# A separate block of minus ones for the norm's second matmul, at an address 16 bytes past the others, and 15 KB less scratch ahead of the tiles

## Chip, core and metric

The kernel runs on one core of a Trainium2 chip. The metric is device microseconds (us) of one execution, the median of several runs. One further execution was taken with the hardware profiler; all rows below come from it. The engines are PE (TensorE, with PEld for its weight loads), DVE (VectorE), ACT (ScalarE), POOL (GpSimd) and SP (SyncE, which here issues the transfers).

## What is computed

A decoder trunk of four layers on 256 tokens of width 1024, in float32. Each layer is a half-weighted gated feed-forward block, a token mixer (three kinds in turn), and a second half-weighted feed-forward block. Each block starts with an RMS norm. The reference, cut:

```python
def rms_norm(x, g):
    y = x * lax.rsqrt(jnp.mean(x * x, axis=-1, keepdims=True) + EPS)
    return y * g

def swiglu(x, w_gate_up, w_down):
    g, u = jnp.split(x @ w_gate_up, 2, axis=-1)
    return (jax.nn.silu(g) * u) @ w_down

for i in range(4):                                   # D_MODEL 1024, D_FF 2816
    h = h + 0.5 * swiglu(rms_norm(h, norm_ffn1[i]), ffn1_w_gate_up[i], ffn1_w_down[i])
    hn = rms_norm(h, norm_mix[i])
    h = h + (stick_breaking, moba, mla)[i % 3](hn)
    h = h + 0.5 * swiglu(rms_norm(h, norm_ffn2[i]), ffn2_w_gate_up[i], ffn2_w_down[i])
return rms_norm(h, final_norm)
```

## The kernel before

**Split operands.** Every large matrix product is made of three products of rounded parts. A weight chunk is loaded by SP into a `raw` tile, ACT writes its rounded high part into one of six `whi` tiles (L318), DVE writes the rest, the low part, into one of six slots of the tile `wlo` (L325). The activations are split in the same way: `x2` holds, for each of 8 blocks of 128 features, 256 high and then 256 low values a row; `a2` holds the same for the 22 blocks of the feed-forward block's inner width.

**The wide pair.** In the feed-forward blocks the three products are two matmuls (function `wide`, L475 and L476). The first holds a high weight block of 128x128 in the array and streams 512 columns, the high and low activations side by side. The second holds the low weight block and streams the 256 high columns. A feed-forward block has 22 x 16 such pairs in its gate-and-up part (`gate_up`) and 8 x 22 in its down part, 528 in all, and there are eight blocks: 4224 pairs. While one matmul streams, the array's next weight block is loaded (PEld).

**Other products.** The mixers' projections use three matmuls of 256 columns (`mm3`, L469 to L471, weights high, high, low), or three of up to 512 columns in which the activations are the held operand (`x_proj`, L516 to L518).

**The norm of a feed-forward block** (`norm_rows`). ACT and DVE split the sum of squares `acc` into a high and a low half, `parted`, the last block of `a2`. PE then sums over the 128 partitions with a block of minus ones: L441 streams all 512 columns, L442 streams the 256 low columns once more, both with the same block `full` held. DVE takes the inverse root from the result (L447 to L453). The pair L441, L442 stands in PE's order some 24 pairs after the start of a feed-forward block, since a block's first products need the norm only when they leave PSUM. There are eight such pairs in the program. `full` is also held in the stick-breaking mixer (L667).

**Addresses.** [...] In the built program `whi` starts at byte 49280, `full` at 73856, `x2` at 74432, `a2` at 90816, `wlo` at 135872: each a multiple of 64. The six low slots, however, begin 4 values, 16 bytes, into `wlo`:

```python
lows = cp.tile([P, 4 + 6 * HALF], F32R, name="wlo")
parts = Slots([(whi[i], lows[:, 4 + i * HALF:4 + (i + 1) * HALF]) for i in range(6)])
```

So a high weight block, `full` and all streamed rows begin at a multiple of 64 bytes, and a low weight block begins 16 bytes past one. A block of 128 values is 512 bytes, so in each slot the blocks lie 512 bytes apart.

**Order.** A small scheduler (class `Program`) fixes the order of the instructions on each engine when the kernel is built, from costs written in the code.

Of the kernel before, what the change touches and what calls it, by code (L numbers as in the profile page):

```python
# [11 lines left out]
F32R = mybir.dt.float32r  # L12
# [3 lines left out]
ALU = mybir.AluOpType  # L16
AX = mybir.AxisListType

P = 128
D = 1024  # L20
SEQ = 256
# [18 lines left out]
HALF = MAXC // 2  # L40
# [155 lines left out]
def trunk_kernel(ctx: ExitStack, tc: tile.TileContext, a: dict, out: bass.AP, nsub: int = 3 * DEPTH):  # L196
    nc = tc.nc
    ctx.enter_context(tc.manual_schedule())
    cp = ctx.enter_context(tc.tile_pool(name="consts", bufs=1))
# [21 lines left out]
    def room(n, shape, name, dt=F32):  # L221
        return Slots([cp.tile([P] + shape, dt, name=f"{name}{i}") for i in range(n)])
# [5 lines left out]
    whi = [cp.tile([P, HALF], F32R, name=f"whi{i}") for i in range(6)]  # L228
    full = cp.tile([P, P], F32R, name="full")
# [1 line left out]

    x2 = cp.tile([P, NT, 2, SEQ], F32R, name="x2")
    a2 = cp.tile([P, NF, 2, SEQ], F32R, name="a2")
    lows = cp.tile([P, 4 + 6 * HALF], F32R, name="wlo")
    parts = Slots([(whi[i], lows[:, 4 + i * HALF:4 + (i + 1) * HALF]) for i in range(6)])
    mids = room(3, [2 * ZC], "mid")
    probs = room(2, [2, ZC], "prob")
    nats = room(5, [512], "nat")
# [20 lines left out]
    def bank(keep=0):  # L259
        return Buf(psum, keep)  # L260
# [10 lines left out]
    identf = cp.tile([P, P], F32, name="identf")  # L271
# [9 lines left out]
    nc.vector.tensor_scalar(neg_sb, jp, 0.0, NEG, op0=ALU.is_le, op1=ALU.mult)  # L281
    nc.vector.tensor_scalar(neg_sm, jp, 0.0, NEG, op0=ALU.is_gt, op1=ALU.mult)
    nc.vector.tensor_scalar(tri, jp, 0.0, -1.0, op0=ALU.is_le, op1=ALU.mult)
    nc.vector.tensor_scalar(full, identf, 0.0, -1.0, op0=ALU.mult, op1=ALU.add)
    nc.vector.memset(onesf, 1.0)


# [137 lines left out]
    def norm_rows():  # L425


        t, z = Buf(mids), bank()
        lead = 10.0

        parted = a2[:, NF - 1].rearrange("p a b -> p (a b)")
        th, tl, tx = (slice(i * SEQ, (i + 1) * SEQ) for i in range(3))

        def high():
            nc.scalar.activation(parted[:, th], acc, AF.Copy)

        def low():
            nc.vector.tensor_sub(parted[:, tl], acc, parted[:, th].bitcast(F32))

        def sums():  # L440
            nc.tensor.matmul(z.ap, full, parted, start=True, stop=False, skip_group_check=True)  # L441
            nc.tensor.matmul(z.ap[:, :SEQ], full, parted[:, tl], start=False, stop=True, skip_group_check=True)  # L442

        def newton():
            x, y, u = t.ap[:, tx], t.ap[:, th], t.ap[:, tl]

            nc.vector.tensor_scalar(x, z.ap[:, :SEQ], 0.5 / D, -0.5 * EPS, op0=ALU.mult, op1=ALU.add)  # L447
            nc.vector.tensor_scalar(y.bitcast(I32), x.bitcast(I32), -0.5, float(0x1EF759DF), op0=ALU.mult,
                                    op1=ALU.add)
            for i in range(3):  # L450
                nc.vector.tensor_mul(u, y, y)
                nc.vector.tensor_mul(u, u, x)
                nc.vector.scalar_tensor_tensor(rb[:, 0, :] if i == 2 else y, u, 1.5, y, op0=ALU.add, op1=ALU.mult)  # L453

        o = g.act(SEQ, high, [state["acc"]], lead=lead)
        o = g.dve(SEQ, low, [o], lead=lead)
        o = g.op("PE", wide_cost(1), sums, [o], take=[z, t], lead=lead)
        n = g.op("DVE", 11 * 0.4, newton, [o], free=[z, t], lead=lead)
        g.act(SEQ, lambda: nc.scalar.activation(rb[:, 1, :], rb[:, 0, :], AF.Copy, scale=0.5), [n], lead=lead)
        return n  # L460
# [17 lines left out]
    def wide_cost(n):  # L478
        return n * (3 * SEQ / 2400 + 0.005)
# [44 lines left out]
    def ffn(l, which, g_next):  # L524
        gu, dn = a[f"ffn{which + 1}_gu"], a[f"ffn{which + 1}_dn"]
        rms = norm_rows()
        act = [None] * NF
        xdeps = list(state["x"])
# [443 lines left out]
    for m, e in zip(CUTS, CUTS[1:] + [NT]):  # L972
        s = slice(G_ALL + m * SEQ if m else 0, G_ALL + e * SEQ)
        x = g.op("DMA", 0.37 * (e - m), lambda s=s: nc.sync.dma_start(gh[:, s], a["gx"][:, s]), lead=61.0 - 3.0 * m)
# [88 lines left out]
def build(arrays, nsub=3 * DEPTH):  # L1063
    import concourse.bacc as bacc

    nc = bacc.Bacc("TRN2", target_bir_lowering=False, num_devices=1)
    aps = {n: nc.dram_tensor(f"in_{n}", v.shape, mybir.dt.from_np(v.dtype), kind="ExternalInput").ap()
           for n, v in arrays.items()}
    out = nc.dram_tensor("out_0", (SEQ, D), F32, kind="ExternalOutput").ap()
    with tile.TileContext(nc) as tc:  # L1070
        trunk_kernel(tc, aps, out, nsub)
    return nc
# [9 lines left out]
```

## Time and profile before

| | |
|---|---|
| median of 3 runs | 1942.61 us (1941.03 to 1947.96) |
| the profiled execution | 1941.18 us |
| its span, from the first to the last instruction | 1939.3 us |
| mean granted TensorE clock | 0.996 of full speed |
| PE busy, share of the span | 1921.3 us, 99% |
| PEld / DVE / ACT / POOL busy | 87% / 76% / 59% / 0% |
| DMA, mean busy share of 16 engines, HBM read | 50.4% on its main queue, 339.76 MB |

Matmuls overlap: the next one starts while the one before still drains, so a matmul's duration (0.39 us for 512 columns) is longer than the distance to the next start. Rates are read from starts, or from how many matmuls of one line fall into a stretch.

### The profile page before, as it was taken

The numbers are of one execution on the slowest core, as the hardware profiler recorded it, in microseconds if no ns is written. First come the engines' busy times: TensorE is split into PE (matmuls) and PEld (weight loads), VectorE is DVE, ScalarE is ACT, GpSimd is POOL, SyncE is SP. The second block draws the span as 40 slices with busy tenths as digits, with TensorE's granted clock in tenths as the row PEclk, the third lists the DMA queues.
The fourth block names the chain that finished last, engine by engine and source line by source line (L and its number), as shares of the span: only waits on it lengthen the run. The fifth ranks groups of instructions, "written<-read, shape, count | busy, mean of one in ns | idle before, by whom it ended". The sixth has DMA issues, their size and how long they took to land.

```text
span 1939.3 us, 30483 instructions
## 1 busy us (share of the span) xinstructions
PE 1921.3 (99%) x11649; PEld 1683.4 (87%) x11649; DVE 1468.5 (76%) x2669; ACT 1149.3 (59%) x2119; POOL 0.4 (0%) x5
## 2 busy tenths in 40 slices
PE   8999999999999999999999999999999999999997
PEld 7888989888888878888888888988888888998886
DVE  8777668776877777877787778887678767668864
ACT  6565556555665555655566557755556655565553
POOL 0000000000000000000000000000000000000000
PEclk9999999999999999999999999999999999999999
DMA  7546434545654653454555454355465456335542
GB/s 277 196 150 228 167 138 155 193 155 193 217 196 147 226 183 119 161 206 150 199 208 192 154 183 155 127 199 178 154 217 199 173 175 230 131 132 194 182 151 80
DMA packets 55873, 342.77 MB, mean 177 GB/s; under 512 B 6192, under 2 KB 7088, under 8 KB 26928
## 3 DMA queue, kind: packets, MB, share of 16 engines
q1 hardware_dynamic: 55728, 340.84, 50.4%
q8 instruction: 91, 1.49, 0.3%
q14 instruction: 54, 0.44, 0.1%
HBM read 339.76 MB, written 1.05 MB: 176 GB/s over the span
## 4 chain that ended last, share of the span: by engine, by line
PE 98%; DVE 1%; ACT 1%; DMA 0%; issue 0%; SPq 0%; DVEq 0%; ACTq 0%
PE ps L475 50%; PE ps L476 25%; PE ps L469 3%; PE ps L470 3%; PE ps L471 3%; PE ps L516 3%; PE ps L518 2%; PE ps L517 2%; PE ps L615 1%; PE ps L665 1%; PE ps L774 1%; PE ps L739 1%; PE ps L812 1%; PE ps L637 1%; PE ps L603 0%; PE ps L617 0%
## 5 line engine op out<-in xcount | busy, mean ns | idle before, releaser
L318 ACT ACTIVATE whi<-raw 128x1024 fp32r<-128x1024 f32 (+2 forms) x738 | 703.4, 954 | 691.5 <-PE ps L475 486.3
L325 DVE TENSOR_TENSOR wlo<-raw,whi 128x1024 fp32r<-128x1024 f32 (+2 forms) x738 | 802.9, 1090 | 357.8 <-ACT whi L318 344.4
L475 PE MATMUL ps<-x,whi 128*128 128x512 f32 x2816 | 981.0, 394 | 0.7 <-DVE acc L349 0.6
L476 PE MATMUL ps<-x,wlo 128*128 128x256 f32 x2816 | 783.5, 278 | 4.3 <-DVE wlo L325 4.3
L475 PEld LDWEIGHTS ps<-x,whi 128*128 128x128 f32 x2816 | 529.4, 188 | 125.2 <-ACT whi L318 1.9
L476 PEld LDWEIGHTS ps<-x,wlo 128*128 128x128 f32 x2816 | 530.3, 188 | 5.1 <-DVE wlo L325 5.1
L475 PE MATMUL ps<-a,whi 128*128 128x512 f32 x1408 | 489.6, 394 | 0.0
L476 PE MATMUL ps<-a,wlo 128*128 128x256 f32 x1408 | 390.8, 278 | 0.0
L475 PEld LDWEIGHTS ps<-a,whi 128*128 128x128 f32 x1408 | 263.9, 187 | 61.3
L476 PEld LDWEIGHTS ps<-a,wlo 128*128 128x128 f32 x1408 | 264.3, 188 | 0.0
L484 DVE TENSOR_TENSOR mid<-ps,mid 128x256 f32<-128x256 f32 x416 | 172.7, 417 | 12.6 <-ACT mid L483 12.5
L483 ACT ACTIVATE mid<-ps 128x256 f32<-128x256 f32 x416 | 150.7, 366 | 11.4 <-PE ps L476 9.3
L556 DVE TENSOR_TENSOR mid<-mid 128x256 f32<-128x256 f32 x176 | 74.0, 423 | 11.7
L551 DVE TENSOR_TENSOR mid<-mid,rb 128x256 f32<-128x256 f32 x176 | 74.1, 423 | 4.8
L552 ACT ACTIVATE mid<-mid 128x256 f32<-128x256 f32 x176 | 72.0, 410 | 6.6 <-DVE mid L551 6.4
L558 DVE TENSOR_TENSOR a<-mid,a 128x256 fp32r<-128x256 f32 x176 | 73.1, 418 | 2.5 <-ACT a L557 2.4
L516 PE MATMUL ps<-whi,x 128*128 128x512 f32 (+2 forms) x192 | 74.0, 385 | 0.0
L469 PE MATMUL ps<-a,whi 128*128 128x256 f32 x256 | 73.8, 288 | 0.0
L469 PE MATMUL ps<-x,whi 128*128 128x256 f32 x256 | 73.1, 285 | 0.0
L518 PE MATMUL ps<-whi,x 128*128 128x512 f32 (+2 forms) x192 | 72.8, 379 | 0.0
L517 PE MATMUL ps<-wlo,x 128*128 128x512 f32 (+2 forms) x192 | 72.3, 377 | 0.0
L471 PE MATMUL ps<-x,wlo 128*128 128x256 f32 x256 | 71.9, 281 | 0.0
(141 smaller groups left out, 1658.0 us busy)
## 6 DMA issues: line engine op xcount, KB each, us to landing
raw<-in_ffn_gu SPq DMA_DIRECT2D x173, 1024.0 KB, 4.8
raw<-in_ffn_dn SPq DMA_DIRECT2D x128, 704.0 KB, 4.0
raw<-in_sb_qk SPq DMA_DIRECT2D x16, 1024.0 KB, 4.8
raw<-in_moba_qkv SPq DMA_DIRECT2D x12, 1024.0 KB, 4.8
raw<-in_sb_v SPq DMA_DIRECT2D x8, 1024.0 KB, 4.7
raw<-in_sb_o SPq DMA_DIRECT2D x8, 1024.0 KB, 4.7
raw<-in_moba_o SPq DMA_DIRECT2D x4, 1024.0 KB, 4.7
raw<-in_mla_o SPq DMA_DIRECT2D x4, 1024.0 KB, 5.0
```

The lines of the kernel that those rows point to most:

```text
L318: return lambda: nc.scalar.activation(b.ap[0][:, (k - i) * w:(e - i) * w], raw.ap[:, k * w:e * w], AF.Copy)
L325: nc.vector.tensor_sub(b.ap[1][:, s], raw.ap[:, k * w:e * w], b.ap[0][:, s].bitcast(F32))
L469: nc.tensor.matmul(o, wh, mh, start=first, stop=False, skip_group_check=True)
L471: nc.tensor.matmul(o, wl, mh, start=False, stop=last, skip_group_check=True)
L475: nc.tensor.matmul(o, wh, m2.rearrange("p a b -> p (a b)"), start=first, stop=False, skip_group_check=True)
L476: nc.tensor.matmul(o[:, :SEQ], wl, m2[:, 0, :], start=False, stop=last, skip_group_check=True)
L483: x = g.act(SEQ, lambda: nc.scalar.activation(o(), b.ap[:, SEQ:], AF.Copy), [last], take=take, lead=lead)
L484: return g.dve(SEQ, lambda: nc.vector.tensor_add(o(), b.ap[:, :SEQ], o()), [x], free=[b], lead=lead)
L516: nc.tensor.matmul(o, xs[0][:, k, ts], hi, start=(k == 0), stop=False)
L517: nc.tensor.matmul(o, xs[0][:, k, ts], lo, start=False, stop=False)
L518: nc.tensor.matmul(o, xs[1][:, k, ts], hi, start=False, stop=(k == n - 1))
L551: o = g.dve(SEQ, lambda: nc.vector.tensor_mul(x(), x(), rb[:, 0, :]), [o, rms])
```

## The change

Two things. The tile `wlo` becomes 128 values longer. Its first 128 values behind the 16 bytes are a second block of minus ones, `full_lo`, written once at the start by DVE; the six low slots move 512 bytes up. The norm's second matmul holds `full_lo` in place of `full`. And the framework's scratch area is set to 1 KB in place of 16 KB.

```diff
-    lows = cp.tile([P, 4 + 6 * HALF], F32R, name="wlo")
-    parts = Slots([(whi[i], lows[:, 4 + i * HALF:4 + (i + 1) * HALF]) for i in range(6)])
+    lows = cp.tile([P, 4 + P + 6 * HALF], F32R, name="wlo")
+    full_lo = lows[:, 4:4 + P]
+    parts = Slots([(whi[i], lows[:, 4 + P + i * HALF:4 + P + (i + 1) * HALF]) for i in range(6)])
...
-    nc.vector.tensor_scalar(full, identf, 0.0, -1.0, op0=ALU.mult, op1=ALU.add)
+    for x in (full, full_lo):
+        nc.vector.tensor_scalar(x, identf, 0.0, -1.0, op0=ALU.mult, op1=ALU.add)
...
             nc.tensor.matmul(z.ap, full, parted, start=True, stop=False, skip_group_check=True)
-            nc.tensor.matmul(z.ap[:, :SEQ], full, parted[:, tl], start=False, stop=True, skip_group_check=True)
+            nc.tensor.matmul(z.ap[:, :SEQ], full_lo, parted[:, tl], start=False, stop=True, skip_group_check=True)
...
-    nc = bacc.Bacc("TRN2", target_bir_lowering=False, num_devices=1)
+    nc = bacc.Bacc("TRN2", target_bir_lowering=False, num_devices=1, dynamic_dma_scratch_size=1024)
```

In the built program every tile up to and with the start of `wlo` lies 15,360 bytes lower, and every tile behind `wlo` 14,848 bytes lower; both are multiples of 512, so no tile's place within 512 bytes changes. Each low slot starts 14,848 bytes lower, 16 bytes past a multiple of 64 as before.

On PE the order of the instructions is the same. Here is the first norm's place in PE's order, before (the names after `<-` are the streamed tile and the held one, `ps` is a PSUM bank):

```order
L475 MATMUL ps_71<-x_86,whi_82 128x512
L476 MATMUL ps_71<-x_86,wlo 128x256
L441 MATMUL ps_72<-a_87,full 128x512
L442 MATMUL ps_72<-a_87,full 128x256
L475 MATMUL ps_70<-x_86,whi_82 128x512
L476 MATMUL ps_70<-x_86,wlo 128x256
```

And with the change, in which lines are numbered three higher here:

```order
L478 MATMUL ps_71<-x_86,whi_82 128x512
L479 MATMUL ps_71<-x_86,wlo 128x256
L444 MATMUL ps_72<-a_87,full 128x512
L445 MATMUL ps_72<-a_87,wlo 128x256
L478 MATMUL ps_70<-x_86,whi_82 128x512
L479 MATMUL ps_70<-x_86,wlo 128x256
```

Nothing moved; the second matmul of the norm reads its held block from `wlo`. The other seven norms read alike.

On DVE one instruction is added, among the constants that are written at the start. Before:

```order
L283 TENSOR_SCALAR tri<-acc 128x128
L284 TENSOR_SCALAR full<-identf 128x128
L285 MEMSET onesf 128x2
L360 SCALAR_TENSOR_TENSOR x_86<-gh,x_86 128x256
L325 TENSOR_TENSOR wlo<-raw_74,whi_78 128x256
```

With the change:

```order
L284 TENSOR_SCALAR tri<-acc 128x128
L286 TENSOR_SCALAR full<-identf 128x128
L286 TENSOR_SCALAR wlo<-identf 128x128
L287 MEMSET onesf 128x2
L362 SCALAR_TENSOR_TENSOR x_86<-gh,x_86 128x256
L327 TENSOR_TENSOR wlo<-raw_74,whi_78 128x256
```

The second L286 is new; everything behind it on DVE is one place later. ACT, POOL and SP have the same instructions in the same order.

## Rows read from the trace of the kernel before

**Rows 1.** The page's chain that ended last, by engine and by line.

```profile
PE 98%; DVE 1%; ACT 1%; DMA 0%; issue 0%; SPq 0%; DVEq 0%; ACTq 0%
PE ps L475 50%; PE ps L476 25%; PE ps L469 3%; PE ps L470 3%; PE ps L471 3%; PE ps L516 3%; PE ps L518 2%; PE ps L517 2%; PE ps L615 1%; PE ps L665 1%; PE ps L774 1%; PE ps L739 1%; PE ps L812 1%; PE ps L637 1%; PE ps L603 0%; PE ps L617 0%
```

**Rows 2.** L475 by stretch: stretch, its us, busy (matmuls), granted clock, DMA.

```profile
36.35:192.69 156.34, 156.34 (x460) 1.00 0.57 199
...
507.84:674.38 166.54, 166.54 (x490) 1.00 0.55 190
```

**Rows 3.** The same view, four other stretches.

```profile
321.20:507.70 186.50, 186.16 (x527) 1.00 0.53 186
801.30:989.20 187.90, 187.47 (x531) 1.00 0.54 190
1266.00:1452.50 186.50, 186.08 (x527) 1.00 0.53 186
1749.30:1878.70 129.40, 129.22 (x366) 1.00 0.50 172
```

**Rows 4.** PE in order of time at the second norm: start, duration, line.

```profile
320.55 0.39 PE L475 MATMUL ps<-x,whi 128*128 128x512 f32 x1
...
320.89 0.39 PE L441 MATMUL ps<-a,full 128*128 128x512 f32 x1
321.11 0.28 PE L442 MATMUL ps<-a,full 128*128 128x256 f32 x1
321.23 0.40 PE L475 MATMUL ps<-x,whi 128*128 128x512 f32 x1
...
321.58 0.40 PE L475 MATMUL ps<-x,whi 128*128 128x512 f32 x1
```

**Rows 5.** PE in order of time at the third norm.

```profile
506.38 0.40 PE L441 MATMUL ps<-a,full 128*128 128x512 f32 x1
...
507.44 0.39 PE L475 MATMUL ps<-x,whi 128*128 128x512 f32 x1
...
507.78 0.39 PE L475 MATMUL ps<-x,whi 128*128 128x512 f32 x1
```

**Rows 6.** PE where the first mixer ends and a feed-forward block begins.

```profile
311.34 0.39 PE L475 MATMUL ps<-x,whi 128*128 128x512 f32 x1
...
312.39 0.39 PE L475 MATMUL ps<-x,whi 128*128 128x512 f32 x1
...
312.73 0.39 PE L475 MATMUL ps<-x,whi 128*128 128x512 f32 x1
```

**Rows 7.** PE where the first mixer's projections begin, behind a feed-forward block.

```profile
194.74 0.28 PE L469 MATMUL ps<-x,whi 128*128 128x256 f32 x1
...
195.08 0.28 PE L469 MATMUL ps<-x,whi 128*128 128x256 f32 x1
...
195.44 0.28 PE L469 MATMUL ps<-x,whi 128*128 128x256 f32 x1
```

**Rows 8.** PE at the first transposes of the last stage.

```profile
1878.80 0.38 PE L376 MATMUL ps<-identf,nat 128*128 128x128 f32 x2
1878.94 0.48 PE L475 MATMUL ps<-a,whi 128*128 128x512 f32 x1
```

**Rows 9.** PE's longest wait, in the first block (the bracket: idle before, and what ended it).

```profile
29.01 0.58 PE L476 MATMUL ps<-x,wlo 128*128 128x256 f32 x1 [4.12 <-DVE wlo L325]
```

**Rows 10.** DVE at the start.

```profile
1.93 0.22 DVE L284 TENSOR_SCALAR full<-identf 128x128 fp32r<-128x128 f32 x1
...
4.08 0.48 DVE L360 SCALAR_TENSOR_TENSOR x<-gh,x 128x256 fp32r<-128x256 f32 x1 [1.93 <-ACT x L358]
```

**Rows 11.** The page's DMA queues: packets, MB, share of 16 engines.

```profile
q1 hardware_dynamic: 55728, 340.84, 50.4%
q8 instruction: 91, 1.49, 0.3%
q14 instruction: 54, 0.44, 0.1%
```

## The prediction

> **What bounds the kernel.** I read the chain that ended last first: PE has 98% of it, and two lines, L475 and L476, have 75% [rows 1]. So the time is a sum over PE's starts, above all over the 4224 wide pairs, and an edit counts by what it does to the distance between them. The page says that PE is 99% busy, which hides how fast the pairs go. I therefore counted L475 by stretch. A window counts every matmul that reaches into it, so I set the edges where the count is exact to one. In the stretches of rows 2, 490 pairs take 166.54 us (the same in two more such stretches, one in each later layer's first block) and 460 take 156.34 us: 0.340 us a pair. In the stretches of rows 3, 1951 pairs take 690.3 us. Three of them hold one norm pair of 0.35 us besides, so a pair takes (690.3 - 1.1) / 1951 = 0.3533 us. **The same instructions run at two rates, 13.3 ns or 3.9% apart.** [...] The slow stretches are nearly the whole second feed-forward block of each layer, the quick ones the first blocks.
>
> **Where the rate changes.** The edges of rows 3 lie at the norm's two matmuls. At the second norm the starts of L475, L441 and the next L475 are 320.55, 320.89 and 321.23: still 0.34 a pair. From there 321.23 to 321.58 is 0.35, and it stays so for 527 pairs [rows 3, 4]. The third norm does the reverse: L441 starts at 506.38, two pairs later the distance is 0.34 again (507.44 to 507.78) and stays [rows 5, 2]. The other inner edges of rows 3 lie just behind a norm pair in the same way. Nothing else that happens within a feed-forward block changes the rate: chunks, PSUM banks and waits that are met in time pass by in 490 pairs without a step [rows 2].
>
> What is peculiar to the norm pair? Three things: its second held block begins at a multiple of 64 bytes and not 16 past one; it is the block that the first matmul held; and its streamed rows begin 1024 bytes into `parted`. The third I rule out. In the quick stretches low and high blocks lie at every multiple of 512 bytes against streamed rows that step by 2048, so a shift by 1024 is one of the distances that run at 0.340 all the time. The first two come again in `mm3`, which holds a high block twice and then a low one: entering it from the quick rate, the first three matmuls take 0.34 (194.74 to 195.08), the next three 0.36 (195.08 to 195.44) [rows 7]. So two held blocks in a row at the same place within 64 bytes push PE out of the quick rate, at two unlike places. The same push can bring the quick rate back: behind every mixer, whose last projection is `mm3`, the first three pairs take 1.05 us (311.34 to 312.39) and the fourth 0.34 [rows 6]. I read the two rates as two steady rhythms between weight loads and streams; which one holds depends on the last disturbance.
>
> [...]
>
> **The change, part by part.**
> *The norm's second matmul.* With `full_lo` at 16 bytes past a multiple of 64, the norm pair has the wide pair's pattern, held blocks at 0, 16, 0, 16. If that is what counts, it disturbs nothing and the rhythm passes through. Then each second feed-forward block, which starts with the quick rate two or three pairs behind the mixer [rows 6], keeps it, and the next layer's first block inherits it. The gain is the four stretches of rows 3: 1951 x 13.3 ns = **25.9 us**. The bounds of this term are 0 (every norm still flips) and 25.9.
> *The last stage.* Behind 1878.7 the last block has 528 - 366 - 24, some 138 pairs, between which two transposes stand per output block. These disturb the rhythm by themselves, 0.48 us for the L475 behind the first [rows 8]. They run slow today. Bounds: 0 and 138 x 13.3 ns = 1.8 us; I take 0, since a transposed block at other sizes is as unlike the pair as `mm3` is.
> *The eight norm pairs themselves* go from about 0.345 to 0.340 us: below 0.1 us in sum, left out.
> *DVE's extra constant.* As the 0.22 us of its twin [rows 10]. DVE then idles 1.93 us until ACT hands over the first activations [rows 10], so it costs nothing; uncovered it would be 0.22 us once.
> *The scratch.* The core has three queues: the hardware's and two of instructions [rows 11]. [...] What it does is move tiles, by multiples of 512 bytes. By the argument on distances above that changes no pair, so 0; the bound on the other side is the third rival.
> *Waits.* `full_lo` is written once, long ahead of the first norm, and PE's first norm matmul waits already for DVE's later write of `parted`. No engine waits for anything new.
> *The first block.* Before its norm it runs slow, and the norm flips it to quick. That flip is lost, for a few pairs only: PE then waits 4.12 us for weights [rows 9], and the rhythm is set anew behind it. Today it comes out quick, as the first row of its group shows [rows 2]. I take that it does again.
>
> Sum against the profiled execution's own time: 1941.18 - 25.9 = 1915.3 us. That execution lay 1.4 below the median of the three runs shown and 0.15 above the lowest, so I add a little: **1915.5 us**. Its own range, with the last stage and the spread of the runs, is 1913 to 1918.
>
> **Rivals.**
> *The flip isn't the address (no change).* The norm pair flips the rhythm through what I ruled out, or by its mere presence, or the rates have another cause. For it: I can't separate the place of the second held block from other peculiarities of `norm_rows` in the norm's own rows. Against it: rows 7 show a flip with no norm. Time: 1941 us, 1939 to 1943. [...]
> *The first block stays slow.* The wait of rows 9 resets the rhythm by chance, and it comes out slow; without the norm's flip it holds until the mixer. That takes 13.3 ns from some 468 quick pairs (the 460 of rows 2 and the edges), 6.2 us: 1921.5 us. Against it: three restarts after mixers and this one all ended quick.
> *The entry behind the mixers comes out slow (the other side).* The tiles have moved; if the three pairs of rows 6 now settle in the slow rate, no norm flips it back. Such a layer's second block then stays as slow as today, and the next layer's first block, some 500 pairs, is slow too. For one of the first three layers that turns 7.0 us of gain into 7.0 of loss (527 + 500 pairs at 13.3 ns and the 24 pairs ahead of the norm). One such entry gives 1929 us, two about 1943, and from two on the change doesn't pay; with all four it is 1941.2 + 3 x 7.0 + 0.3 = 1962.5 us. Against it: all places within 512 bytes are kept, and the four entries came out alike. For it: I can't tell from the rows why they come out quick.
>
> **How the numbers follow.** Quick throughout 0.67; first block slow 0.08; one slow entry 0.06; no change 0.12; two or more slow entries 0.07. The range 1912 to 1931 holds the first three, 0.81. A change within 0.5% (9.7 us) can't be told from none here: faster by more is 0.67 + 0.08 + 0.06 = 0.81, within it 0.12, slower 0.07.
>
> **What the profile after would show.** Right: L475 counts near 490 in 166.5 us in the second blocks too, starts 0.34 apart on both sides of every norm pair, mean durations of L475 and L476 a little lower, and nothing else moved. A slow entry or a slow first block shows as some 471 in the same time from there on. Wrong would be a flip of the rate at the norm pair in spite of the new block, or flips at places where there were none.

## The result and the profile after

The changed kernel takes 1914.08 us (median of 4 runs, 1912.87 to 1919.24) against 1942.29 us before (4 runs, 1941.03 to 1947.96): the ratio is 0.9854, with a 95% interval from 0.9828 to 0.9881. 1915.5 us was forecast. The profiled execution took 1913.88 us, its span is 1911.8 us, 27.5 less than before. The shares of PE, DVE and ACT on the page barely moved (99%, 77% and 60% now), and the chain is still 98% PE, 75% of it the two lines of the wide pair, which are now L478 and L479.

L478 by stretch, the first row in the first layer's first block, the others in the second blocks of the first three layers (stretch, its us, busy, number of matmuls, granted clock, DMA share, GB/s):

```profile
40.00:190.00 150.00, 150.00 (x442) 1.00 0.58 201
322.30:488.84 166.54, 166.54 (x491) 1.00 0.55 189
806.00:972.54 166.54, 166.54 (x491) 1.00 0.59 203
1264.00:1430.54 166.54, 166.54 (x491) 1.00 0.57 197
```

The second blocks, in which 527 and 531 pairs ran at 0.353 us [rows 3], now fit as many pairs into 166.54 us as the quick stretches of before did, 491 against 490, one more at the edges [rows 2]. PE in order of time at the second norm, which before turned the rate [rows 4]:

```profile
320.97 0.39 PE L478 MATMUL ps<-x,whi 128*128 128x512 f32 x1
...
321.31 0.39 PE L444 MATMUL ps<-a,full 128*128 128x512 f32 x1
321.53 0.28 PE L445 MATMUL ps<-a,wlo 128*128 128x256 f32 x1
321.65 0.39 PE L478 MATMUL ps<-x,whi 128*128 128x512 f32 x1
...
321.99 0.39 PE L478 MATMUL ps<-x,whi 128*128 128x512 f32 x1
```

Four starts 0.34 apart: the norm pair is now one wide pair among the others. At all eight norms the three starts ahead of L444, L444 and the four behind it are 0.34 us apart. The first transposes of the last stage [rows 8], after:

```profile
1853.24 0.38 PE L378 MATMUL ps<-identf,nat 128*128 128x128 f32 x2
1853.37 0.47 PE L478 MATMUL ps<-a,whi 128*128 128x512 f32 x1
...
1853.80 0.39 PE L478 MATMUL ps<-a,whi 128*128 128x512 f32 x1
...
1854.14 0.39 PE L478 MATMUL ps<-a,whi 128*128 128x512 f32 x1
```

The transposes cost once, 0.43 us from 1853.37 to the next L478, and the pair behind the first L478 is back at 0.34. From the first transpose to the last wide pair took 48.7 us before and takes 46.8 us now. DVE's start [rows 10], after:

```profile
1.93 0.22 DVE L286 TENSOR_SCALAR full<-identf 128x128 fp32r<-128x128 f32 x1
2.06 0.22 DVE L286 TENSOR_SCALAR wlo<-identf 128x128 fp32r<-128x128 f32 x1
...
4.08 0.48 DVE L362 SCALAR_TENSOR_TENSOR x<-gh,x 128x256 fp32r<-128x256 f32 x1 [1.79 <-ACT x L360]
```

The new constant takes its time out of DVE's wait, 1.79 us in place of 1.93, and the first activations are split at 4.08 us as before.

The sum closes: 25.9 us in the four stretches, 1.9 in the last stage, less 0.4 in the first layer (its second norm starts at 321.31 and not at 320.89), is 27.4 of the 27.5 us. The 0.4 arise in the first block. Its norm pair starts at 22.12 and not at 20.72; ahead of it, from 11.43 to 14.42 us, the granted clock was 0.50, with pairs 0.64 us apart, and from 12 to 16 us it was 0.68, where it was 1.00 before. PE had waited 1.18 us for a weight block shortly before the clock fell, at 9.64 us; its wait at that place, 9.53 us, was 0.58 us before the change. Some 1.0 of the 1.4 us have come back where the first mixer starts, at 195.15 and not at 194.74. What made the clock differ is not shown.

### The profile page after: what moved, and what is told of

It is laid out like the page before. It is cut to its first block, busy times and chain, and to the rows that moved or that the text cites. A ratio compares the mean times of both kernels' runs of the same rounds, so it can differ in the third digit from the quotient of the medians.

```text
span 1911.8 us, 30484 instructions
## 1 busy us (share of the span) xinstructions
PE 1893.1 (99%) x11649; PEld 1674.1 (88%) x11649; DVE 1467.3 (77%) x2670; ACT 1150.4 (60%) x2119; POOL 0.4 (0%) x5
## 4 chain that ended last, share of the span: by engine, by line
PE 98%; DVE 1%; ACT 1%; DMA 0%; SPq 0%; issue 0%; DVEq 0%; ACTq 0%
PE ps L478 50%; PE ps L479 25%; PE ps L472 3%; PE ps L473 3%; PE ps L474 3%; PE ps L519 3%; PE ps L521 2%; PE ps L520 2%; PE ps L618 1%; PE ps L668 1%; PE ps L777 1%; PE ps L742 1%; PE ps L815 1%; PE ps L640 1%; PE ps L606 0%; PE ps L620 0%
## 5 line engine op out<-in xcount | busy, mean ns | idle before, releaser
L478 PE MATMUL ps<-x,whi 128*128 128x512 f32 x2816 | 962.3, 390 | 1.4 <-ACT whi L320 1.4
L479 PE MATMUL ps<-x,wlo 128*128 128x256 f32 x2816 | 779.3, 277 | 4.4 <-DVE wlo L327 4.4
L478 PEld LDWEIGHTS ps<-x,whi 128*128 128x128 f32 x2816 | 530.1, 188 | 113.2 <-ACT whi L320 2.7
L479 PEld LDWEIGHTS ps<-x,wlo 128*128 128x128 f32 x2816 | 530.0, 188 | 5.6 <-DVE wlo L327 5.5
L478 PE MATMUL ps<-a,whi 128*128 128x512 f32 x1408 | 480.1, 389 | 0.0
L479 PE MATMUL ps<-a,wlo 128*128 128x256 f32 x1408 | 388.6, 276 | 0.0
L478 PEld LDWEIGHTS ps<-a,whi 128*128 128x128 f32 x1408 | 264.3, 188 | 54.7
L479 PEld LDWEIGHTS ps<-a,wlo 128*128 128x128 f32 x1408 | 264.3, 188 | 0.0
L560 ACT ACTIVATE a<-mid 128x256 fp32r<-128x256 f32 x176 | 70.6, 404 | 2.4 <-DVE mid L559 1.9
```

The lines of the kernel that those rows point to most:

```text
L478: nc.tensor.matmul(o, wh, m2.rearrange("p a b -> p (a b)"), start=first, stop=False, skip_group_check=True)
L479: nc.tensor.matmul(o[:, :SEQ], wl, m2[:, 0, :], start=False, stop=last, skip_group_check=True)
```

## The experiments

All are timed against the kernel before. "Flips" are changes of the wide pair's distance between 0.340 and 0.353 us at a norm pair. The theories: **A**, as the prediction had it, a held block's place within 64 bytes, two at the same place in a row disturb; **B**, the moved tiles; **C**, the very same block held twice in a row; **D**, the region of memory, ahead of or behind the activations; **E**, the place, but within more than 64 bytes. D and E were formed on the way.

**e1_scratch_only.** The kernel before with one edit:

```diff
-    nc = bacc.Bacc("TRN2", target_bir_lowering=False, num_devices=1)
+    nc = bacc.Bacc("TRN2", target_bir_lowering=False, num_devices=1, dynamic_dma_scratch_size=1024)
```

> The kernel before with the scratch at 1 KB alone: all tiles 15,360 bytes lower, the norm's two matmuls as before. Theory A (the place of the norm's second held block within 64 bytes): the rate of the wide pairs flips at the eight norm pairs as before, four slow stretches of some 527, 531, 527 and 366 pairs at 0.353 us and the last stage slow, about 1941 us. Rival B (the moved tiles did it): quick at 0.340 us throughout, about 1914 us.

1942.99 us, ratio 0.999 (0.9976 to 1.0003). L475 came 502 times from 333 to 510 us, in the first layer's second block, and 472 times from 520 to 680 us, in the block behind the third norm: 0.353 and 0.339 us a pair, as in the kernel before. B falls: the smaller scratch gains nothing by itself.

The profiled execution of e1 is one of the long ones, 1949.37 us. In it the first block runs at 0.353 us a pair. L475 from 40 to 190 us, where the kernel before has 443 matmuls:

```profile
40.00:190.00 150.00, 150.00 (x425) 1.00 0.54 189
```

**e2_block_at_0.** The second block of minus ones at the first byte of `wlo`, not 16 bytes in:

```diff
-    full_lo = lows[:, 4:4 + P]
+    full_lo = lows[:, 0:0 + P]
```

> The changed kernel, with the second block of minus ones a tile region of its own, but at a multiple of 64 bytes; the low slots stay 16 bytes past one. Theory A (the place within 64 bytes): the flips come back at the norm pairs, 1939 to 1943 us. Rival C (what disturbs is that the very same block is held twice in a row): no flips, about 1914 us. Rival B (moved tiles): no flips, about 1914 us.

1915.12 us, ratio 0.9847 (0.982 to 0.9875), and no flip at the second norm: L444 starts at 319.59 us, L478 behind it at 319.93, 320.27 and 320.61. **Theory A falls**: this block lies at a multiple of 64 bytes, as `full` does.

**e3_swapped.** The norm's two held blocks in the other order:

```diff
-            nc.tensor.matmul(z.ap, full, parted, ...)
-            nc.tensor.matmul(z.ap[:, :SEQ], full_lo, parted[:, tl], ...)
+            nc.tensor.matmul(z.ap, full_lo, parted, ...)
+            nc.tensor.matmul(z.ap[:, :SEQ], full, parted[:, tl], ...)
```

> The changed kernel with the norm's two held blocks in the other order: first the one 16 bytes past, then the one at a multiple of 64. Held places around the norm are then 0, 16, 16, 0, 0, 16. Theory A in the form 'two held blocks in a row at the same place disturb': there are two such places, the flips come back, about 1941 us (or another pattern of flips, 1920 to 1965). Rival C (same block twice): no flips, about 1914 us.

1913.23 us, ratio 0.9846 (0.9815 to 0.9877). PE at the second norm, and L478 in the block behind it:

```profile
320.55 0.40 PE L444 MATMUL ps<-a,wlo 128*128 128x512 f32 x1
320.78 0.28 PE L445 MATMUL ps<-a,full 128*128 128x256 f32 x1
320.89 0.39 PE L478 MATMUL ps<-x,whi 128*128 128x512 f32 x1
...
321.23 0.39 PE L478 MATMUL ps<-x,whi 128*128 128x512 f32 x1
```

```profile
322.00:488.54 166.54, 166.54 (x491) 1.00 0.54 188
```

The L444 takes 0.23 us to the next start in place of 0.22, and the quick rate goes on, 491 matmuls in 166.54 us. A's form "two in a row at the same place disturb" fails here too. C was still alive. Note for later that the second held block is `full` here, and nothing flips.

**e4_one_flip.** `full` held twice again, in one norm alone:

```diff
-    def norm_rows():
+    def norm_rows(second=full_lo):
...
-        rms = norm_rows()
+        rms = norm_rows(full if l == 0 and which == 1 else full_lo)
```

> The changed kernel with the old held block in the norm of one block alone, the second feed-forward block of the first layer. If the rhythm is inherited until something disturbs it, that norm flips to the slow rate, nothing flips it back until the second layer's mixer: some 527 + 500 pairs at 0.353 us, 13.7 us more, about 1928 us, and the rest of the kernel quick. If each block chose its rate by itself: 527 pairs alone, 7 us, about 1921 us. If only the moved tiles count: 1914 us.

1927.09 us, ratio 0.9909 (0.9884 to 0.9933). L478 by stretch, the first layer's second block, the second layer's first block, the second layer's second block:

```profile
321.50:506.00 184.50, 184.50 (x523) 1.00 0.54 187
508.00:684.00 176.00, 176.00 (x499) 1.00 0.53 186
812.00:980.00 168.00, 168.00 (x496) 1.00 0.56 195
```

That is 0.353, 0.353 and 0.339 us a matmul. One norm pair sets the rate for some 363 us, through the next block with another norm pair in it, until the mixer. **The rhythm is inherited**, and the price is 13.0 us where 13.7 were expected.

**e5_both_lo.** `full_lo` held in both of the norm's matmuls:

```diff
-            nc.tensor.matmul(z.ap, full, parted, ...)
+            nc.tensor.matmul(z.ap, full_lo, parted, ...)
```

> The changed kernel with both of the norm's matmuls holding the block that lies 16 bytes past a multiple of 64, so the same block twice as before the change, but at the other place. Theory C (holding the very same block twice in a row disturbs the rhythm, wherever it lies): the rate flips at the norms, four slow stretches again, about 1941 us (or a partial pattern, 1920 to 1965). Rival D (what counts is that the second block lies in the region of the low blocks, behind the activations): no flips, about 1914 us.

1913.43 us, ratio 0.9835 (0.9814 to 0.9857). PE at the second norm:

```profile
325.95 0.39 PE L444 MATMUL ps<-a,wlo 128*128 128x512 f32 x1
326.19 0.28 PE L445 MATMUL ps<-a,wlo 128*128 128x256 f32 x1
326.30 0.39 PE L478 MATMUL ps<-x,whi 128*128 128x512 f32 x1
...
326.65 0.39 PE L478 MATMUL ps<-x,whi 128*128 128x512 f32 x1
...
326.99 0.39 PE L478 MATMUL ps<-x,whi 128*128 128x512 f32 x1
```

The norm pair and the pair behind it take 0.35, then 0.34 again. The same block twice disturbs, but the rhythm comes back to the quick one. C falls as the cause of the lasting flip.

**e6_beside_full.** The second block as a tile directly behind the first, with the low tile again as before the change:

```diff
     full = cp.tile([P, P], F32R, name="full")
+    full_lo = cp.tile([P, P], F32R, name="full2")
```

> The changed kernel with the second block of minus ones as a tile of its own directly behind the first, at a multiple of 64 bytes, far from the low blocks; the activations move 512 bytes up, the low slots are as before the change. Theory C (same block twice): no flips, about 1914 us. Rival D (region of the low blocks): flips, about 1941 us.

1941.66 us, ratio 0.9992 (0.9977 to 1.0007): the flip is back at the second norm (L444 at 320.04 us, L478 at 320.38, 320.73 and 321.09), with a block of its own that is held once. L478 behind the second norm, 0.353 us a pair:

```profile
330.00:500.00 170.00, 170.00 (x482) 1.00 0.54 191
```

C falls a second time. D stood, but one thing had been overlooked: in the built program `whi`, `full` and this block begin at byte 128 of 512, while `x2`, `a2` and `wlo`, behind 64 bytes of padding (the tile `shift`), begin at byte 192. So place (E) and region (D) still went together.

**e9_lows_class_full** and **e10_beside_class_lows** part them. In e9 the block lies among the low slots, but at byte 128 of 512; in e10 it lies beside `full`, but at byte 192.

The edit of e9, with which the slots begin 512 bytes later:

```diff
-    lows = cp.tile([P, 4 + P + 6 * HALF], F32R, name="wlo")
-    full_lo = lows[:, 4:4 + P]
-    parts = Slots([(whi[i], lows[:, 4 + P + i * HALF:4 + P + (i + 1) * HALF]) for i in range(6)])
+    lows = cp.tile([P, 4 + 2 * P + 6 * HALF], F32R, name="wlo")
+    full_lo = lows[:, 112:112 + P]
+    parts = Slots([(whi[i], lows[:, 4 + 2 * P + i * HALF:4 + 2 * P + (i + 1) * HALF]) for i in range(6)])
```

The edit of e10, with the low tile again as before the change; the padding now lies inside the new tile:

```diff
     full = cp.tile([P, P], F32R, name="full")
-    cp.tile([P, 16], F32, name="shift")
+    full_lo = cp.tile([P, 16 + P], F32R, name="full2")[:, 16:]
```

> The changed kernel with the second block of minus ones still ahead of the low slots, but moved so that it stands at byte 128 of 512, as the first block and the high blocks do (the activations and the low tile begin at byte 192 of 512, 64 further). Low slots at their old place within 512. Theory E (the place counts, but within more than 64 bytes: a second held block at the high blocks' place disturbs): flips come back, 1939 to 1943 us. Rival D (the region of the low blocks counts, behind the activations): no flips, 1913 to 1916 us.

> The second block as a tile directly behind the first, far from the low blocks, but 64 bytes further within 512, at byte 192, where the activations and the low tile begin; all other places within 512 are as in the changed kernel. Theory E: no flips, 1913 to 1916 us. Rival D: flips, 1939 to 1943 us.

e9: 1941.41 us, ratio 0.9996 (0.9983 to 1.0009). PE at its second norm:

```profile
320.73 0.39 PE L444 MATMUL ps<-a,full 128*128 128x512 f32 x1
320.95 0.28 PE L445 MATMUL ps<-a,wlo 128*128 128x256 f32 x1
321.07 0.40 PE L478 MATMUL ps<-x,whi 128*128 128x512 f32 x1
...
321.42 0.40 PE L478 MATMUL ps<-x,whi 128*128 128x512 f32 x1
...
321.78 0.40 PE L478 MATMUL ps<-x,whi 128*128 128x512 f32 x1
```

e10: 1916.83 us, ratio 0.9873 (0.9852 to 0.9894). PE at its second norm (here the wide pair is L477, L478):

```profile
322.04 0.39 PE L443 MATMUL ps<-a,full 128*128 128x512 f32 x1
322.27 0.28 PE L444 MATMUL ps<-a,full 128*128 128x256 f32 x1
322.38 0.39 PE L477 MATMUL ps<-x,whi 128*128 128x512 f32 x1
...
322.72 0.39 PE L477 MATMUL ps<-x,whi 128*128 128x512 f32 x1
```

In e9 the distance goes to 0.35 and 0.36, and the time is that of the kernel with the flips; in e10 it stays 0.34. **The place within 512 bytes decides, not the region**: behind `full`, which lies at byte 128, a second block at byte 128, where the high blocks are, flips the quick rate; one at byte 192 or 208 doesn't. The second block's place alone is not the rule, though: in e3 it is at byte 128, behind a first one at 208, and nothing flips. All the norm pairs that turned the quick rate have both blocks at byte 128.

From the slow rate the pairs behave otherwise. The slow rate passes the pair with a second block at 208 unchanged (e4's third norm, with 0.353 us on both sides; e8 below). In e10, with 192, PE reaches the first norm pair at the slow rate and runs at the quick one from the fourth start behind it; this is a single case, in which the region differs as well:

```profile
22.16 0.40 PE L477 MATMUL ps<-x,whi 128*128 128x512 f32 x1
...
22.51 0.40 PE L477 MATMUL ps<-x,whi 128*128 128x512 f32 x1
...
22.87 0.40 PE L443 MATMUL ps<-a,full 128*128 128x512 f32 x1
...
24.25 0.39 PE L477 MATMUL ps<-x,whi 128*128 128x512 f32 x1
...
24.59 0.39 PE L477 MATMUL ps<-x,whi 128*128 128x512 f32 x1
```

**e7_lows_at_0.** All low slots and `full_lo` without the 16 bytes:

```diff
-    lows = cp.tile([P, 4 + P + 6 * HALF], F32R, name="wlo")
-    full_lo = lows[:, 4:4 + P]
-    parts = Slots([(whi[i], lows[:, 4 + P + i * HALF:4 + P + (i + 1) * HALF]) for i in range(6)])
+    lows = cp.tile([P, 0 + P + 6 * HALF], F32R, name="wlo")
+    full_lo = lows[:, 0:0 + P]
+    parts = Slots([(whi[i], lows[:, 0 + P + i * HALF:0 + P + (i + 1) * HALF]) for i in range(6)])
```

> The changed kernel with all low slots and the second block of minus ones at a multiple of 64 bytes, so no held block anywhere is 16 bytes past one. If the 16 bytes bear on the quick rate (theory A's rest): the 4224 wide pairs run at 0.353 us or slower, 55 us more or above, 1969 us. If only holding the same block twice counts (theory C): 0.340 us, about 1914 us.

1916.65 us, ratio 0.9853 (0.9834 to 0.9872), and 489 matmuls of L478 from 322 to 488 us, 0.339 us each: the wide pairs' quick rate doesn't need the 16 bytes. The time lies some 2.6 us above the changed kernel's, of runs that overlap; I don't claim a difference.

**e11_no_shift** and **e12_shift_128.** The padding ahead of `x2` taken out, and doubled; the activations and the low tile then begin at byte 128 and at byte 256 of 512.

```diff
# e11
-    cp.tile([P, 16], F32, name="shift")
# e12
-    cp.tile([P, 16], F32, name="shift")
+    cp.tile([P, 32], F32, name="shift")
```

> The changed kernel without the 64 bytes of padding between the block of minus ones and the activations: activations and low tile then begin at byte 128 of 512 like the high blocks, and the low slots and the second block lie 16 bytes past that. If the quick rate rests on high and low held blocks lying 64 (80) bytes apart within 128 (theory E's reason): no quick rate, the 4224 wide pairs at 0.353 us or slower, 1965 us or above. If only the norm's second block counts for the rate: 1914 us.

> The changed kernel with 128 bytes of padding between the block of minus ones and the activations in place of 64: activations and low tile begin at byte 256 of 512, high blocks and the first block of minus ones at 128 as ever, the low slots 16 bytes past 256. Without padding the pairs ran at one rate of 0.3467 us. If a place counts within 128 bytes, this kernel is like that one: 0.3467 us a pair, about 1944 us. If it counts within 256 or 512 bytes, the rate is another: at 0.340 us or better the time is 1914 us or less, and that would be a version to keep.

e11: 1943.96 us, ratio 1.0005 (0.999 to 1.0019). e12: 1967.51 us, ratio 1.0128 (1.011 to 1.0147), slower than both kernels. The wide pair's first line by stretch, first e11 (L477), then e12 (L478):

```profile
332.00:510.00 178.00, 178.00 (x515) 1.00 0.54 190
```

```profile
332.00:512.00 180.00, 180.00 (x513) 1.00 0.54 186
```

e11 has a third rate, 0.3467 us a pair from start to start, and e12 a fourth, 0.352 (the counts give 0.346 and 0.351, with a matmul too many at the edges); both have the same rate on the two sides of the third norm (e11 434 matmuls in 150 us from 530 us on, e12 455 in 160). In e11's first block, from 40 to 190 us, L477 came 425 times, 0.353 us a pair: this kernel has two rates as well. So of the three paddings only 64 bytes has the 0.340 us, and 128 bytes, with 0.352, are not the same as none, with 0.3467.

**e8_mm3_order.** In the mixers' projections the three matmuls of a step in another order:

```diff
         nc.tensor.matmul(o, wh, mh, start=first, ...)
-        nc.tensor.matmul(o, wh, ml, ...)
-        nc.tensor.matmul(o, wl, mh, ..., stop=last, ...)
+        nc.tensor.matmul(o, wl, mh, ...)
+        nc.tensor.matmul(o, wh, ml, ..., stop=last, ...)
```

> The changed kernel with the three matmuls of a projection step in the order high, low, high weights in place of high, high, low, so that the same block is never held twice in a row there (a step ends and the next begins with high blocks, but different ones, both at a multiple of 64 bytes). Theory C: the 512 triples go from some 0.354 to 0.340 us, 7 us less, about 1907 us. Theory A (same place within 64 bytes in a row): no gain, 1914 us.

1962.41 us, ratio 1.0088 (1.0069 to 1.0107): slower, which neither theory expected. The triples stayed at 0.35 us (309.96 to 310.31 us at the end of the first mixer; 310.99 to 311.34 before). PE where the first mixer ends (the same place as [rows 6]):

```profile
310.55 0.28 PE L474 MATMUL ps<-a,whi 128*128 128x256 f32 x1
310.66 0.40 PE L478 MATMUL ps<-x,whi 128*128 128x512 f32 x1
...
311.02 0.40 PE L478 MATMUL ps<-x,whi 128*128 128x512 f32 x1
...
311.37 0.40 PE L478 MATMUL ps<-x,whi 128*128 128x512 f32 x1
...
311.72 0.40 PE L478 MATMUL ps<-x,whi 128*128 128x512 f32 x1
```

With a high block as the last one of the mixer, the feed-forward block starts in the slow rate, and the norm pairs don't turn it: L478 came 522 times from 322 to 506 us, 499 times from 508 to 684, behind the third norm, and 505 times from 1286 to 1464, behind the third mixer, 0.353 us a pair each time. This is the prediction's third rival, brought about by another edit: 1962.5 us was its price with four slow entries, 1962.4 is measured.

## Why the prediction was right, and where its reason was not

**The two rates and the flips** were read rightly: two steady distances, 0.340 and 0.353 us, that change at the norm pair; the change removes all eight flips. The granted clock is 1.00 at both rates, before [rows 2, 3] and after, and DMA is 0.54 busy at the slow one from 801.30 to 989.20 us [rows 3] and at a quick one (L475 in the kernel before):

```profile
989.44:1155.98 166.54, 166.54 (x490) 1.00 0.54 183
```

So neither of the two parts the rates.

**The size** 1951 x 13.3 ns = 25.9 us held; e4 gives the price of a single slow run independently, 13.0 us for some 1027 pairs, 12.7 ns each. **Inheritance** from block to block, on which the gain in later layers and the third rival rest, is shown by e4 (0.353 us up to 684 us, behind a second norm pair) and e8 (0.353 up to 684 us as well).

**The step that failed is the cause of the flip.** The prediction said that two held blocks in a row at the same place within 64 bytes push PE out of the quick rate. e2 has the second block at a multiple of 64, like `full`, and stays quick; e3 and e5 have two blocks in a row at the same place and keep or regain the quick rate. What the runs showed in its place: a norm pair with both held blocks at byte 128 of 512 flips the quick rate (the kernel before, e1, e4, e6, e9); with one of the two at 192 or 208 it doesn't (the changed kernel, e2, e7, e10, e3), and with both at 208 it disturbs two pairs and no more (e5). The 16 bytes of the edit are not what helps; that the block moved into the low tile, 64 bytes further within 512, is. The forecast came out because the edit did both, and that was luck: the same reason had e2 gain nothing, and e2 gained as much. The argument by which I dropped larger distances compared only streamed and held rows that step by 512; it never looked at the place within 512, where the kernel before held `full` and the high blocks at 128 and everything else at 192 or 208.

**The last stage** was mis-sized: 0 was taken, 1.8 was the bound, 1.9 us came. The transposes don't push the pairs out of the quick rate: it is 0.34 again from the second start behind them. The stage has 134 pairs and not 138, since 28 and not 24 pairs stand ahead of the last norm; that is below 0.1 us.

**DVE's constant and the scratch** cost nothing, as taken: the constant's 0.22 us lie in DVE's wait, and e1, with 1 KB of scratch alone, took 1942.99 us. No run shows what the scratch is used for; that its size is worth 0 within the interval is what e1 measured (ratio 0.9976 to 1.0003).

**The first block** came out quick in the profile after (442 matmuls in 150 us), as taken. The rival that it stays slow is real all the same. In the profiled execution of e5 the same stretch is:

```profile
40.00:190.00 150.00, 150.00 (x426) 1.00 0.54 190
```

That execution took 1918.48 us, and the other three of e5 1912.92 to 1913.55 us: 5 to 6 us apart, near the 6.2 us of that rival. This stretch lies behind PE's longest wait [rows 9]. The kernel before and the changed one are quick in it (443 and 442 matmuls), e5 and e1 are slow (426 and 425; e1's execution took 1949.37 us), so the block can come out either way, and no run shows what decides. The run of 1919.24 us of the changed kernel and that of 1947.96 us before lie as far above the others, but have no trace; that this is their cause too is argued.

**What stays open** is why. The runs show that the place of held blocks within 512 bytes turns the distance between matmuls, at which places, and that e11 and e12 differ; e11 and e12 move the streamed rows and the low blocks together, so they don't tell which of the two counts. That the two rates are rhythms between weight loads and streams was the author's reading; no run shows it, nor why byte 128 twice flips and byte 208 twice doesn't, nor with how many bytes the pattern repeats.

## What to carry to other kernels

Before trusting that an engine at 99% is at its rate, divide stretches by counts: the same instructions may run at two distances, here 0.340 and 0.353 us, and the place of the step shows where to look for its cause. Look at the full addresses of held and streamed tiles in the built program, not only at the offset that a line of code adds; a 64-byte pad between tiles was worth 1.5% here (e11 against the changed kernel), and a single odd pair of matmuls set the rate of the thousand pairs behind it (e4, 13.0 us). When an edit changes two things at once (16 bytes and a tile), try each apart, even when the forecast comes out.

## What was unexpected of the hardware

The wide pair has discrete rates, 0.340, 0.3467, 0.352 and 0.353 us in these kernels, all at a granted clock of 1.00. One pair of matmuls can turn it, or let it pass, by where its two held blocks lie within 512 bytes: with both at 128 the distance went from 0.34 to 0.35 and 0.36 (e9), with the second at 192 it stayed 0.34 (e10). Between 0.340 and 0.353 the choice is a memory of the past: e4 kept one for 363 us. Another order of the three matmuls of the mixers' projections (e8) cost 48 us against the changed kernel though those matmuls themselves took the same 0.35 us a triple.
